# A Conformer trunk on one core: norms in one piece, a sixth plain chunk, pooling tiles as slices, ScalarE's tables asked for early

## The chip, the cores and the metric

The kernel runs on one core of one Trainium2 chip. The metric is the device time of an execution in microseconds; the median of three runs before the change is 1699.82 us (1695.87 to 1700.03). The core has TensorE (PE, with its weight loads shown as PEld), VectorE (DVE), ScalarE (ACT), GpSimd (POOL) and a DMA-issuing queue SP; each engine works off its own queue in order.

## The reference, cut to what matters

528 tokens (16 meta tokens and 512 frames) of 1024 channels pass through two Conformer layers, all in float32. The first layer mixes tokens by pooling, the second by latent attention over a key/value computed between the layers. Every sub-layer begins with an RMS norm.

```python
def rmsnorm(x, g):  x * rsqrt(mean(x*x, -1) + 1e-6) * g
def swiglu(h, w_gate, w_up, w_down):  (silu(h @ w_gate) * (h @ w_up)) @ w_down    # 1024 -> 2816 -> 1024
# layer l
h = h + 0.5 * swiglu(rmsnorm(h, ffn1_norm[l]), ...)
u = rmsnorm(h, mix_norm[l])
h = h + pool_mixer(u, pool_w, pool_scale)       # l == 0: trailing means over 2, 4, 8, 16 tokens
                                                # minus the token, a 256x256 map per channel group
h = h + mla_attention(u, ...)                   # l == 1: 8 heads, chunk-causal softmax(q k^T) v
h = h + 0.5 * swiglu(rmsnorm(h, ffn2_norm[l]), ...)
# after layer 0: shared k, v from rmsnorm(h, kv_in_norm); at the end rmsnorm(h, final_norm), meta dropped
```

## The kernel before, in words

Activations lie with channels on the 128 partitions and tokens along the free dimension: `h` is eight tiles of 128 x 528. Each float32 operand of a matmul is split in two fp32r parts, a high one (a rounded copy, made by ScalarE) and a low one (the remainder, made by VectorE); a product takes three matmuls, high x high, high x low and low x high (`mm3`, L193; `plain`, L371; `product`, L383). A weight of 512 KB comes from DRAM to a `raw` tile (two buffers), ScalarE copies its high part (L169), VectorE subtracts the remainder (L170), and the pair goes to two of 14 `w` tiles. `tp` holds 48 tiles of 128 x 528 for everything else.

The four feed-forwards (`ffn`) go over 22 chunks of 128 hidden units. A chunk's gate and up are made in one of two ways. *Plain* (`gate_up_plain`): 96 matmuls, from weights brought whole and split. *In sums* (`gate_up`): a Strassen-like scheme with 84 matmuls; it needs sums of weight halves, which DMA engines add on the way in (`bring_sums`: two loads on SP and an accumulating one on POOL) and VectorE completes (`add_up`, L421 and L422), and sums of halves of the input (`sums_x`, L245 to L248 and two splits for each of four channel pairs). `prepare` splits the forms of a chunk one ahead. Blocks of four or three chunks are then multiplied by the down weights, eight steps to a block (`down_steps`), put between the three slots of the chunks in sums of the following block; the last block's steps come at the end, and each step adds to one `h` tile (L614, L617).

Three feed-forwards have a norm of their own (`first_chunks`): chunk 0 runs on the unnormalised input and is scaled afterwards, so that the mean squares can be computed beside it. `rms[0]` makes the mean squares (L275), their powers on POOL and diagonal tiles (L292, L294); `rms[1]` broadcasts them (L303, L307). Chunk 1 still runs on the unnormalised input; `normal_x` (L224, then L183/L184 for the split) makes the normalised input piece by piece, from which chunk 2 on is computed, and from which `sums_x` is made. Before, chunks 0 to 4 are plain (`begun = 5`). The third feed-forward gets its normalised input from outside (`first_chunk`): the norm's broadcast is shared with the key/value projection (L811 to L829), its chunks 0 and 1 are plain.

The pooling mixer first applies the 256x256 maps (`z_products`, L734: tokens of tile j as the stationary operand), scales by the norm (`z_parts`, L740 and L741; mean squares in `z_scale`, L715), then applies band matrices over tokens (L766 to L778), adding to `h` at L780. Tokens come in tiles of 128; a fifth tile of 80 rows (`x5`, filled by POOL casts at L695, and `s5`) held the last 16 tokens of each half, apart from each other, in two groups.

Attention is one list of steps (`ATTENTION`): keys and queries of a head, values of a token tile, the scale for the scores (`scales`, L897 to L907), scores with their exponential (L990), normalising, transposing (`turn`, L1047) and weighing (L1065).

The order in which an engine runs its instructions is set when the kernel is built: a planner walks the program with its own model of times and issues, on each engine, what it holds to be ready, earlier lines first. So lines written later can come ahead of earlier ones that it thinks are not ready. ScalarE loads a function table when an activation of another set of functions comes up (Copy and Square need none of their own).

Of the kernel before, what the change touches and what calls it, by code (L numbers as in the profile page):

```python
# [11 lines left out]
F32 = mybir.dt.float32  # L12
# [46 lines left out]
B_0, B_4, B_M, NB = 0, 256, 528, 928  # L59
# [5 lines left out]
keys 0, values 1, scales, queries 0, values 3, queries 1, scores3 0, scores2 0, values 2, scores10 0, values 0,  # L65
# [15 lines left out]


def tail(ap):

    return ap.rearrange("p (a b) -> p a b", b=NM)[:, 15::17, :]


def spread(ap):

    return ap.rearrange("p (a b) -> p a b", b=64)[:, :, :NM]  # L90
# [3 lines left out]
def trunk(ctx: ExitStack, tc, h0, wall, vecs, band, rope, out):  # L94
# [26 lines left out]

    def psum():
        return psp.tile([P, 512], F32, tag="ps", name=name("ps"))
# [11 lines left out]
    nc.scalar.activation(warm, warm, AF.Copy)  # L135
# [45 lines left out]
    def split_to(dst, src):  # L181

        nc.scalar.activation(dst[0], src, AF.Copy)  # L183
        nc.vector.tensor_tensor(dst[1], src, dst[0], op=ALU.subtract)  # L184
# [33 lines left out]
    def normal_x(xs, c, g, t0, r):  # L218
# [112 lines left out]
    def fetch_gate_up(u0, one=fetch):  # L331
        one(u0)
        one(u0 + 1)

    def ffn(u0, x, g, rms, t0, after, early=None, final=None, normed=None, hooks=()):
# [56 lines left out]

        def pair_of_sums():
            return sump.tile([P, 2, 512], F32, tag="sum", name=name("sum"))
# [136 lines left out]
        def first_chunks():  # L531

            nonlocal x
# [16 lines left out]
            plain(w_g, pg, halves)  # L550
            r = rms[1]()
            fetch_gate_up(u0 + 6)
# [6 lines left out]
            fetch_gate_up(u0 + 9)  # L559
            sums_x(x, 0)  # L560
            gate_up_plain(2, True)
            fetch_gate_up(u0 + 12)
            sums_x(x, 1)
            sums_x(x, 2)
            gate_up_plain(3)
            bring_sums(5)
            bring(5)
            evacuate(0, *held, r)
            sums_x(x, 3)
            bring_sums(6)  # L570
            gate_up_plain(4, pair=True)
            prepare(5)
            bring(6)

        def first_chunk():
# [6 lines left out]
            for k in range(2):  # L582
                sums_x(x, k)
            gate_up_plain(1)
            for k in range(2, 4):
                sums_x(x, k)
            prepare(2)
# [38 lines left out]
        begun = 5 if normed is None else 2  # L626
# [42 lines left out]
    rows = [P, P, P, P, 80]  # L669
    x5, bands = [], []  # L670

    def early():
# [11 lines left out]
        for i in range(2):  # L684
            x5.append((slot(F32R)[:, :512], slot(F32R)[:, :512]))
            for t in x5[i]:
                nc.gpsimd.memset(t.bitcast(F32), 0.0)

    done = prep([(xm, V_MIX, 0)], ssq_m, 0)

    def after(c):
        done(c)
        for e in range(2):
            t = x5[c // 4][e][:, (c % 4) * P : (c % 4) * P + P]
            nc.gpsimd.tensor_copy(spread(t), tail(xm[c][e]))  # L695
# [5 lines left out]
    s5 = slot()[:, :P]  # L701
    nc.gpsimd.memset(s5, 0.0)
    nc.vector.tensor_copy(spread(s5), tail(ssq_m))

    def tokens(j, c, e):
        if j == 4:
            return x5[c // 4][e][:, (c % 4) * P : (c % 4) * P + 80]
        return xm[c][e][:, j * P : (j + 1) * P]

    def z_scale():  # L710

        ps = psum()
        for j in range(5):
            sj = s5[:, :80] if j == 4 else ssq_m[:, j * P : (j + 1) * P]
            nc.tensor.matmul(ps[: rows[j], 2 * j : 2 * j + 2], sj, ones_d, start=True, stop=True)  # L715
        v, rc = small(5), small(5)
        nc.vector.memset(v, 1.0)
        nc.vector.tensor_scalar(v[:, :4], ps[:, 0:8:2], EPS, None, op0=ALU.add)
        nc.vector.tensor_scalar(v[:80, 4:5], ps[:80, 8:9], EPS, None, op0=ALU.add)
# [563 lines left out]
```

## Time and profile before

| | before |
|---|---|
| median of three runs | 1699.82 us |
| the profiled execution's own time / its span | 1702.0 / 1700.2 us |
| mean granted TensorE clock | 0.981 |
| PE busy | 1637.3 us (96%), 11976 matmuls |
| DVE busy | 1142.5 us (67%) |
| ACT busy | 809.5 us (48%) |
| POOL busy | 221.9 us (13%) |
| read from HBM | 208 MB, 124 GB/s |

The span runs from the first to the last instruction of the profiled execution; its own time is 1.8 us longer. Busy times are sums over the span. Matmuls overlap their weight loads, and their ends are modelled. A granted clock of 1.00 is TensorE at 2.4 GHz; 0.5 would be 1.2 GHz throughout.

### The profile page before, as it was taken

To read this page: it belongs to the slowest core of one execution; us is meant where nothing else is said; L and a number is where in the kernel's file an instruction comes from. 1 tells how busy PE (TensorE), PEld (TensorE's weight loads), DVE (VectorE), ACT (ScalarE), POOL (GpSimd) and SP (SyncE) were. 2 spreads that over 40 slices of the span, in tenths; PEclk is the share of its full clock that TensorE was granted. 3 is DMA by queue.
4 is the path that set the end of the run, shared out by engine and by line. 5 is a ranking of instruction groups with operands and counts; after the bars stand their busy time and mean duration, and the time that the engine had idled before them with its cause. 6 is when DMAs were issued, how large, how long until landed. Compare 5 with 4: busy or idle time off the path is not lost.

```text
span 1700.2 us, 30059 instructions
## 1 busy us (share of the span) xinstructions
PE 1637.3 (96%) x11976; PEld 1555.5 (91%) x11976; DVE 1142.5 (67%) x1851; ACT 809.5 (48%) x1489; POOL 221.9 (13%) x257
## 2 busy tenths in 40 slices
PE   7999999998999999999899999999899899999997
PEld 7899999997999999999899999898787798999897
DVE  6865666657776566657767667566787766666655
ACT  6543444446454444445454444445576453444443
POOL 2000000005200000002000000001454100000002
PEclk9999999997999999999999999999899899999998
DMA  7455465533244555534355565643102434565411
GB/s 250 112 137 149 139 160 139 141 111 109 75 113 137 148 146 136 138 101 149 88 135 150 153 145 152 152 126 111 50 14 75 124 96 132 142 160 148 134 56 61
DMA packets 166206, 212.20 MB, mean 125 GB/s; under 512 B 10288, under 2 KB 102576, under 8 KB 166064
## 3 DMA queue, kind: packets, MB, share of 16 engines
q1 hardware_dynamic: 146176, 172.60, 32.2%
q0 software_dynamic: 19312, 37.23, 13.3%
q8 instruction: 94, 1.54, 0.4%
q10 hardware_dynamic: 576, 0.43, 0.1%
q14 instruction: 48, 0.39, 0.1%
HBM read 208.12 MB, written 2.10 MB: 124 GB/s over the span
## 4 chain that ended last, share of the span: by engine, by line
PE 84%; DVE 8%; DMA 3%; ACT 3%; issue 1%; POOL 0%; SPq 0%; DVEq 0%; ACTq 0%; POOLq 0%
PE ps L383 41%; PE ps L193 32%; PE ps L371 7%; DMA raw<-wall 2%; DVE t L184 2%; DVE t L224 1%; DVE w L170 1%; PE ps L1065 1%; DMA half<-wall 1%; ACT w L183 1%; DVE w L184 1%; PE ps L978 1%; PE ps L734 0%; PE ps L933 0%; ACT t L990 0%
## 5 line engine op out<-in xcount | busy, mean ns | idle before, releaser
L383 PE MATMUL ps<-t,w 128*128 128x256 f32 (+1 forms) x5964 | 757.1, 283 | 7.9 <-ACT t L525 6.7
L383 PEld LDWEIGHTS ps<-t,w 128*128 128x128 f32 x5964 | 740.1, 188 | 21.0 <-ACT t L525 8.1
L193 PE MATMUL ps<-t,w 128*128 128x264 f32 (+2 forms) x3672 | 628.4, 322 | 6.6 <-ACT t L183 2.0
L193 PEld LDWEIGHTS ps<-t,w 128*128 128x128 f32 x3672 | 527.9, 188 | 54.3 <-ACT t L183 5.0
L183 ACT ACTIVATE w<-half 128x512 fp32r<-128x512 f32 (+1 forms) x263 | 154.6, 603 | 230.8 <-PE ps L383 122.4
L371 PE MATMUL ps<-t,w 128*128 128x264 f32 (+1 forms) x1632 | 222.0, 297 | 21.5 <-DVE t L184 10.1
L371 PEld LDWEIGHTS ps<-t,w 128*128 128x128 f32 x1632 | 211.7, 199 | 30.1 <-DVE t L184 15.0
L403 POOL DMA_DIRECT2D sum<-wall x71 | 86.2, 1215 | 1077.9 <-DMA sum<-wall 400.6
L183 ACT ACTIVATE w<-sum 128x1024 fp32r<-128x1024 f32 x142 | 149.9, 1057 | 161.1 <-PE ps L383 108.2
L184 DVE TENSOR_TENSOR w<-half,w 128x512 fp32r<-128x512 f32 (+1 forms) x263 | 168.4, 655 | 70.6 <-ACT w L183 69.0
L184 DVE TENSOR_TENSOR w<-sum,w 128x1024 fp32r<-128x1024 f32 x142 | 173.1, 1220 | 54.3 <-PE ps L383 36.8
L614 DVE SCALAR_TENSOR_TENSOR h<-ps,h 128x528 f32<-128x528 f32 (+1 forms) x160 | 111.6, 697 | 140.1 <-PE ps L193 139.8
L183 ACT ACTIVATE t<-t 128x528 fp32r<-128x528 f32 (+4 forms) x174 | 99.0, 593 | 115.8 <-DVE t L526 62.9
L521 DVE TENSOR_TENSOR t<-ps,t 128x256 f32<-128x256 f32 (+1 forms) x71 | 30.3, 427 | 139.4 <-PE ps L383 138.5
L184 DVE TENSOR_TENSOR t<-t,t 128x528 fp32r<-128x528 f32 (+4 forms) x174 | 109.3, 643 | 11.2 <-ACT t L183 9.9
L184 DVE TENSOR_TENSOR w<-raw,w 128x1024 fp32r<-128x1024 f32 x71 | 86.7, 1221 | 28.1 <-PE ps L383 20.5
L183 ACT ACTIVATE w<-raw 128x1024 fp32r<-128x1024 f32 x71 | 74.9, 1055 | 55.5 <-PE ps L383 26.0
L170 DVE TENSOR_TENSOR w<-raw,w 128x1024 fp32r<-128x1024 f32 (+1 forms) x52 | 67.3, 1297 | 22.7 <-ACT w L169 21.1
L169 ACT ACTIVATE w<-raw 128x1024 fp32r<-128x1024 f32 (+1 forms) x55 | 54.5, 994 | 54.3 <-DMA raw<-wall 23.1
L263 POOL TENSOR_TENSOR t<-t,t 128x528 f32<-128x528 f32 (+1 forms) x33 | 52.9, 1603 | 156.4 <-ACT t L262 99.1
L513 ACT ACTIVATE t<-ps 128x256 f32<-128x256 f32 (+1 forms) x71 | 27.3, 385 | 81.8 <-PE ps L383 81.2
L211 DVE SCALAR_TENSOR_TENSOR t<-h,vt,t 128x528 fp32r<-128x528 f32 (+1 forms) x48 | 52.2, 1107 | 6.3 <-ACT t L210 6.1
(167 smaller groups left out, 1080.5 us busy)
## 6 DMA issues: line engine op xcount, KB each, us to landing
raw<-wall SPq DMA_DIRECT2D x118, 512.0 KB, 3.4
half<-wall SPq DMA_DIRECT2D x199, 256.0 KB, 3.8
sum<-wall SPq DMA_DIRECT2D x142, 256.0 KB, 3.2
sum<-wall POOLq DMA_DIRECT2D x71, 512.0 KB, 7.0
half<-wall SPq DMA_DIRECT2D x64, 192.0 KB, 2.8
h<-h SPq DMA_DIRECT2D x8, 264.0 KB, 5.6
raw<-wall SPq DMA_DIRECT2D x8, 256.0 KB, 4.0
raw<-band SPq DMA_DIRECT2D x4, 464.0 KB, 4.1
```

The source lines that it names most:

```text
L169: nc.scalar.activation(wh[:, a:b], raw[:, a:b], AF.Copy)
L170: low.tensor_tensor(wl[:, a:b], raw[:, a:b], wh[:, a:b], op=ALU.subtract)
L183: nc.scalar.activation(dst[0], src, AF.Copy)
L184: nc.vector.tensor_tensor(dst[1], src, dst[0], op=ALU.subtract)
L193: nc.tensor.matmul(ps, w[a], x[b][:, c0:c1], start=first and n == 0, stop=last and n == 2)
L211: nc.vector.scalar_tensor_tensor(xl, src, gain(g + c), xh, op0=ALU.mult, op1=ALU.subtract)
L263: (nc.vector if last else nc.gpsimd).tensor_tensor(ssq, ssq, sq, op=ALU.add)
L371: nc.tensor.matmul(ps, w[a][:, k * P : k * P + P], xs[k][i][b], start=k == 0 and n == 0, stop=k == KC - 1 and n == 2,)
L383: nc.tensor.matmul(ps, w[a][:, k * P : k * P + P], xs[k][b], start=first and k == 0 and n == 0, stop=last and k == 3 and n == 2, skip_grou ...
L403: nc.gpsimd.dma_start(t, up[:, :512].unsqueeze(1).to_broadcast([P, 2, 512]), accum_op=ALU.add)
L521: add(u[:, first], pd, u[:, first], op=ALU.add)
L614: nc.vector.scalar_tensor_tensor(hv, at, 0.5, hv, op0=ALU.mult, op1=ALU.add)
```

## The change

- ScalarE: the first instruction asks for Silu instead of Copy; a one-column Exp is added after the last square ahead of attention and a one-column Silu after the last residual of attention. They write a scratch tile.
- Pooling: the token tiles are the slices 0-128, 128-256, 240-368, 368-496 and 496-528 of the activations themselves; the casts, zeroed tiles and the copy of squares go; the band matrices have matching rows and columns.
- Feed-forwards with a norm: six plain chunks (`begun = 6`); the broadcast of the norm stands six eighths into chunk 1's gate. Everything traced after chunk 1's evacuation goes into a `tc.issue_after` block.
- Third feed-forward, pooling, attention: `tc.issue_after` blocks too. `with tc.issue_after(ins)` puts each instruction of the block that runs on the engine of `ins` behind `ins` in that engine's queue; it binds the order of issue on this one engine and nothing else. `xs["low"]`, `low` are VectorE instructions (the last remainder of the normalised input, of the pooled parts), `last` is a TensorE one (the last matmul of the score scale).
- Attention's list: `scales` moves from the third place to behind `values 3`, ahead of `queries 1`.

```diff
-keys 0, values 1, scales, queries 0, values 3, queries 1, scores3 0, scores2 0, values 2, scores10 0, values 0,
+keys 0, values 1, queries 0, values 3, scales, queries 1, scores3 0, scores2 0, values 2, scores10 0, values 0,
-    nc.scalar.activation(warm, warm, AF.Copy)
+    nc.scalar.activation(warm, warm, AF.Silu)
@@ normal_x
-            split_to(p, xn)
+            _, xs["low"] = split_to(p, xn)
@@ first_chunks
-            plain(w_g, pg, halves)
+            plain(w_g, pg, halves, range(6))
             r = rms[1]()
+            plain(w_g, pg, halves, range(6, KC))
             fetch_gate_up(u0 + 6)
             xs = new_x()
             for c in range(KC):
                 normal_x(xs, c, g, t0, r)
             plain(w_u, pu, halves)
             evacuate(1, by_halves(pg), by_halves(pu), r)
             x = xs
-            fetch_gate_up(u0 + 9)
...
-            gate_up_plain(3)
-            bring_sums(5)
-            bring(5)
-            evacuate(0, *held, r)
-            sums_x(x, 3)
-            bring_sums(6)
-            gate_up_plain(4, pair=True)
-            prepare(5)
-            bring(6)
+            with tc.issue_after(xs["low"].ins):
+                fetch_gate_up(u0 + 9)
+                sums_x(x, 0)
+                gate_up_plain(2, True)
+                fetch_gate_up(u0 + 12)
+                sums_x(x, 1)
+                sums_x(x, 2)
+                gate_up_plain(3)
+                fetch_gate_up(u0 + 15)
+                sums_x(x, 3)
+                gate_up_plain(4)
+                evacuate(0, *held, r)
+                bring_sums(6)
+                bring(6)
+                bring_sums(7)
+                gate_up_plain(5, pair=True)
+                prepare(6)
+                bring(7)
@@ first_chunk
+            with tc.issue_after(x["low"].ins):
+                for k in range(2):
+                    sums_x(x, k)
+                gate_up_plain(1)
+                for k in range(2, 4):
+                    sums_x(x, k)
+                prepare(2)
-        begun = 5 if normed is None else 2
+        begun = 6 if normed is None else 2
@@ pooling
-    rows = [P, P, P, P, 80]
+    spans = [(0, P), (P, 2 * P), (240, 368), (368, 496), (496, L)]
+    rows = [b - a for a, b in spans]
-            nc.gpsimd.tensor_copy(spread(t), tail(xm[c][e]))
     def tokens(j, c, e):
-        if j == 4:
-            return x5[c // 4][e][:, (c % 4) * P : (c % 4) * P + 80]
-        return xm[c][e][:, j * P : (j + 1) * P]
+        return xm[c][e][:, slice(*spans[j])]
-    fetch(U_FFN2_0, 2)
-    fetch(U_FFN2_0 + 1, 2)
+    with tc.issue_after(low.ins):
+        fetch(U_FFN2_0, 2)
+        fetch(U_FFN2_0 + 1, 2)
-        b_2, b_3 = bm[:, P : P + 272], bm[:, :272]
-        b_4 = b04[:80, B_4 : B_4 + 272]
+        b_2, b_3 = bm[:, P + 16 : P + 288], bm[:, 16:288]
+        b_4 = b04[: rows[4], B_4 : B_4 + 272]
@@ ahead of attention, in query_scales, behind attention
+    nc.scalar.activation(warm, ssq_c[:, :1], AF.Exp, scale=0.0)
-            nc.tensor.matmul(ps[:, 8 + 2 * j : 10 + 2 * j], ssq_c[:, ts], ones_q, start=True, stop=True)
+            last = nc.tensor.matmul(ps[:, 8 + 2 * j : 10 + 2 * j], ssq_c[:, ts], ones_q, start=True, stop=True)
+        order.enter_context(tc.issue_after(last.ins))
+    nc.scalar.activation(warm, h[KC - 1][:, NM : NM + 1], AF.Silu, scale=0.0)
```

## Rows read from the trace of the kernel before

**Rows 1.** The page's first part: busy us (share of the span) and instructions.

```profile
PE 1637.3 (96%) x11976; PEld 1555.5 (91%) x11976; DVE 1142.5 (67%) x1851; ACT 809.5 (48%) x1489; POOL 221.9 (13%) x257
```

**Rows 2.** Busy by stretch: us; PE, PEld, DVE, ACT, POOL; clock; DMA share; GB/s.

```profile
31.20:60.10 28.90, 23.77 (x152) 21.72 (x152) 25.06 (x47) 13.59 (x22) 1.24 (x1) 0.88 0.51 146
...
382.60:418.10 35.50, 27.45 (x167) 25.61 (x167) 27.53 (x36) 20.48 (x32) 20.43 (x25) 0.76 0.36 115
418.10:441.70 23.60, 23.60 (x197) 23.56 (x195) 17.56 (x28) 13.51 (x23) 9.52 (x6) 1.00 0.07 24
441.70:466.90 25.20, 24.70 (x196) 23.86 (x194) 21.57 (x47) 10.07 (x21) 2.42 (x2) 1.00 0.45 125
...
817.50:840.50 23.00, 17.81 (x110) 15.97 (x110) 22.32 (x50) 7.92 (x19) 1.74 (x2) 0.85 0.28 70
...
1336.50:1366.70 30.20, 25.73 (x147) 22.55 (x146) 25.75 (x51) 12.20 (x23) 1.28 (x1) 0.77 0.32 86
```

**Rows 3.** Chain of waits, first feed-forward: start us, us, what.

```profile
82.95 11.68 PE ps L383 x96
```

**Rows 4.** Timeline of PE, third feed-forward: start, us, engine, line, operation, count.

```profile
839.57 12.56 PE L371 MATMUL ps<-t,w 128*128 128x256 f32 x104
```

**Rows 5.** Timeline of the first feed-forward's norm.

```profile
31.16 6.60 PE L371 MATMUL ps<-t,w 128*128 128x264 f32 x52
...
33.95 0.76 DVE L224 SCALAR_TENSOR_TENSOR t<-h,vt,t 128x528 f32<-128x528 f32 x1
```

**Rows 6.** VectorE by line and shape, 31.2 to 60.1: count | busy, mean ns | idle.

```profile
L170 DVE TENSOR_TENSOR w<-raw,w 128x1024 fp32r<-128x1024 f32 x5 | 6.1, 1222 | 4.5 <-ACT w L169 4.5
L224 DVE SCALAR_TENSOR_TENSOR t<-h,vt,t 128x528 f32<-128x528 f32 x8 | 6.1, 760 | 0.0
L184 DVE TENSOR_TENSOR t<-t,t 128x264 fp32r<-128x264 f32 x8 | 3.2, 426 | 0.0
L184 DVE TENSOR_TENSOR t<-t,t 128x528 fp32r<-128x528 f32 x4 | 2.8, 698 | 0.0
...
L245 DVE TENSOR_TENSOR t<-t 128x264 f32<-128x264 f32 x4 | 1.7, 425 | 0.0
```

**Rows 7.** Chain of waits, fourth feed-forward.

```profile
1357.98 31.66 PE ps L371 x244
```

**Rows 8.** Timelines of PE and of VectorE there; in brackets idle time before, releaser.

```profile
1336.54 5.90 PE L371 MATMUL ps<-t,w 128*128 128x256 f32 x48
...
1339.15 0.69 DVE L421 TENSOR_TENSOR sum<-sum,raw 128x512 f32<-128x512 f32 x1 [3.45 <-DMA raw<-wall]
```

**Rows 9.** Timeline of PE, pooling.

```profile
389.11 2.34 PE L193 MATMUL ps<-t,w 128*128 128x264 f32 x18
...
403.47 1.87 PE L715 MATMUL ps<-ones_d,t 128*128 128x2 f32 x8 [2.54 <-DVE t L263]
...
418.20 0.28 PE L766 MATMUL ps<-t,t 128*128 128x256 f32 x1
```

**Rows 10.** POOL and VectorE by line, 382.6 to 418.1 (pooling).

```profile
L695 POOL CAST t<-t 128x32 fp32r<-128x32 f32 x16 | 10.3, 658 | 21.9 <-ACT t L210 19.7 <-DVE t L211 2.1
...
L170 DVE TENSOR_TENSOR w<-raw,w 128x1024 fp32r<-128x1024 f32 x4 | 6.7, 1678 | 0.3 <-ACT w L169 0.3
...
L170 DVE TENSOR_TENSOR w<-raw,w 128x512 fp32r<-128x512 f32 x4 | 3.6, 929 | 0.3 <-ACT w L169 0.3
```

**Rows 11.** Timeline of the start of attention.

```profile
1210.01 2.94 PE L193 MATMUL ps<-t,w 128*128 128x512 f32 x12
...
1212.80 0.28 PE L898 MATMUL ps<-ones_q,t 128*128 128x2 f32 x2
...
1219.75 1.28 ACT L990 ACT_TABLE_LOAD   x1
...
1221.05 0.79 ACT L990 ACTIVATE t<-ps,s,q 128x528 f32<-128x528 f32 x1
...
1224.67 2.33 PE L978 MATMUL ps<-t,t 128*128 128x256 f32 x9 [3.26 <-ACT t L990]
```

More of the change, by code (lines that the diff above doesn't have):

```diff
@@ L120, in unsplit, with pair_of_sums @@
         return rawp.tile([P, 1024], F32, tag="raw", name=name("raw"))
+    def pair_of_sums():
+        return sump.tile([P, 2, 512], F32, tag="sum", name=name("sum"))
     def psum():
@@ L181, in split_to @@
     def split_to(dst, src):
[L183 to L184 removed]
+        return (
+            nc.scalar.activation(dst[0], src, AF.Copy),
+            nc.vector.tensor_tensor(dst[1], src, dst[0], op=ALU.subtract),
+        )
     def parts(T):
@@ L328, in prep, with fetch_gate_up @@
         return after
-    def fetch_gate_up(u0, one=fetch):
-        one(u0)
-        one(u0 + 1)
+    def fetch_gate_up(u0):
+        fetch(u0)
+        fetch(u0 + 1)
     def ffn(u0, x, g, rms, t0, after, early=None, final=None, normed=None, hooks=()):
@@ L683, in early @@
             bands.append((b04, bm, bl))
[L684 to L694, printed above, removed]
-            nc.gpsimd.tensor_copy(spread(t), tail(xm[c][e]))
+    after = prep([(xm, V_MIX, 0)], ssq_m, 0)
     r0 = ssq
     ffn(U_FFN1_0, x, V_F1, rms_steps([r0], ones_d, L), 0, after, early)
-    s5 = slot()[:, :P]
-    nc.gpsimd.memset(s5, 0.0)
-    nc.vector.tensor_copy(spread(s5), tail(ssq_m))
     def tokens(j, c, e):
-        if j == 4:
-            return x5[c // 4][e][:, (c % 4) * P : (c % 4) * P + 80]
-        return xm[c][e][:, j * P : (j + 1) * P]
+        return xm[c][e][:, slice(*spans[j])]
     def z_scale():
@@ L713, in z_scale @@
         for j in range(5):
-            sj = s5[:, :80] if j == 4 else ssq_m[:, j * P : (j + 1) * P]
-            nc.tensor.matmul(ps[: rows[j], 2 * j : 2 * j + 2], sj, ones_d, start=True, stop=True)
-        v, rc = small(5), small(5)
+            nc.tensor.matmul(ps[: rows[j], 2 * j : 2 * j + 2], ssq_m[:, slice(*spans[j])], ones_d, start=True, stop=True)
+        v, rc, n = small(5), small(5), rows[4]
         nc.vector.memset(v, 1.0)
         nc.vector.tensor_scalar(v[:, :4], ps[:, 0:8:2], EPS, None, op0=ALU.add)
-        nc.vector.tensor_scalar(v[:80, 4:5], ps[:80, 8:9], EPS, None, op0=ALU.add)
+        nc.vector.tensor_scalar(v[:n, 4:5], ps[:n, 8:9], EPS, None, op0=ALU.add)
         for a, b in ((0, 2), (2, 5)):
@@ L1107, in trunk @@
     }
-    for step in ATTENTION.replace("\n", " ").split(","):
-        f, *args = step.split()
-        steps[f](*map(int, args))
+    with ExitStack() as order:
+        for step in ATTENTION.replace("\n", " ").split(","):
+            f, *args = step.split()
+            steps[f](*map(int, args))
     for d in range(KC):
```

33 lines of the change are left out of this document (7 added, 26 removed).

## The prediction

> **What bounds the kernel now.** First the page's busy times: TensorE is busy 1637.3 of 1700.2 us, VectorE 67%, ScalarE 48% [rows 1]. Inside the feed-forwards TensorE runs without gaps; what can be had is the 63 us in which it is idle, and the stretches in which its granted clock is low. Busy time by stretch finds them [rows 2]: the norm of the first feed-forward (TensorE 23.77 of 28.90 us, clock 0.88), the pooling mixer (27.45 of 35.50, clock 0.76), the norm of the third (17.81 of 23.00, 0.85) and of the fourth (25.73 of 30.20, 0.77). In these norms VectorE is the engine that is nearly full (25.06, 22.32, 25.75 us). In the second feed-forward, the same code, TensorE loses only 0.5 us (24.70 of 25.20). The timeline adds the start of attention, where TensorE waits 3.26 us for an exponential [rows 11].
>
> I price a stage by when its successor starts, which counts idle time and slow clock together. The chain of waits gives a matmul's price at full clock: 11.68/96 = 0.122 us with 528 tokens [rows 3], 12.56/104 = 0.120 with 512 [rows 4]. A plain chunk (96) is 11.7 or 11.5 us, a chunk in sums (84) 10.2 or 10.1.
>
> **First feed-forward: norms in one piece, six plain chunks, table.** Before: the plain matmuls end at 82.95; less chunks 3 and 4 (192 x 0.122 = 23.4), chunk 2 ended at 59.5. The chunk in sums behind it puts the start of chunk 6 at 82.95 + 84 x 0.122 = 93.2 [rows 3]. Chunk 1 had its matmuls done at 31.16 + 48 x 0.122 = 37.0 [rows 5], so chunk 2 took 22.5 us for 11.7 of work: it waited for normalised pieces. There VectorE did 6.1 + 3.2 + 2.8 us of norm, and between these the sums (four lines of 1.7), five weight remainders and add-ups [rows 6]. With the block queued behind the last norm remainder, VectorE does from 33.95 [rows 5] 12.1 of norm and the 2 remainders of chunk 2 (2.4), to 48.4; TensorE reaches the last of the eight pieces at 37.0 + 7 x 1.46 = 47.2. The broadcast, emitted 12 matmuls earlier, can bring this up to 1.5 us forward, so the lateness is between 0 and 1.2; I take 0.5. Four plain chunks are 46.8: 84.3. Chunk 3 needs PSUM banks that chunk 1 holds until VectorE evacuates it, now after the norms: 0 to 2 us, I take 1. Chunk 6 starts at 85.3: **-8**. Ends: -10 (no lateness) and -3 (next paragraph).
>
> What is late next is the work put off. From the norms to chunk 6 VectorE has, by the same lines: evacuations of chunks 1 and 0 (2.9 + 2.8), of 2 to 5 (4 x 1.5), six remainders (7.3), sums (10.6), forms of chunk 6 (5.4): 35 us, against 288 x 0.122 = 35.1 of TensorE. It is level. In the second feed-forward's norm VectorE managed 21.57 of 25.20, 86% [rows 2], which would make it 41; but some 6 us of the list (evacuations of 5 and 0, the last forms) isn't wanted when chunk 6 starts. The cover is just there; without it 5 us are lost, which is the -3. Down steps of the first block fall on six slots instead of nine, two to a slot: nothing, TensorE having other products to put between; at worst 2 us a feed-forward for the one pair of banks. SP: the sum loads are for chunks 6 and 7 instead of 5 and 6; chunk 5 brings 1 MB instead of 1.5, POOL issues one summing transfer less.
>
> **Fourth feed-forward, the same edit.** 31.66 us of plain matmuls ran without a gap from 1357.98, to 1389.6 [rows 7]; chunk 2 ended at 1389.6 - 192 x 0.119 = 1366.8. Chunk 1 was done at 1336.54 + 48 x 0.12 = 1342.3. VectorE came late to the norms because an add-up of chunk 5 sat in its queue, waiting 3.45 us for a transfer [rows 8]; that add-up now lies in the block. Wait and add-ups gone, the norms start near 1338, 11.7 us of pieces, to 1349.7, and TensorE wants the last at 1352.4: no lateness. Chunk 6: before 1389.6 + 10.1 = 1399.7, after 1342.3 + 4 x 11.4 = 1387.9, with 2 us for banks and debt 1390: **-9.5** (ends -11.5, -4).
>
> **Second feed-forward.** Half a microsecond to win, and 12 matmuls more: **+1** (0 to +3).
>
> **Third feed-forward.** The first chunk ended 104 - 96 = 8 matmuls after 839.57, at 840.5 [rows 4]. VectorE was full for 22.32 of 23.00 us [rows 2], and sums (6.8), two forms (2.4) and add-ups (1.4) lay between its norms. Without them the chunk ends at 834 to 835. But these 10.6 us are due before the next chunk's 11.5 us are over, and VectorE has other evacuations there, so some 2.5 comes back: **-3.5** (0 to -6).
>
> **Pooling.** 167 matmuls at 0.122 are 20.4 us of the 35.5 [rows 2]: 15 us are lost. The last down step ends at 391.4, the mean squares begin at 403.47 after a wait for the last square, the band matmuls at 418.20 [rows 9]. In between POOL has 16 casts of tails, 10.3 us, in one queue with the six square additions, and VectorE 6.7 + 3.6 us of weight remainders of the next feed-forward [rows 10]. Slices take the casts away; the issue order puts the remainders behind the last pooled part. Then the last residual comes at about 392.4, its split and its square's addition by 396, mean squares and powers 3 to 4 us, the ten parts at 0.65 from 399.9, the last four products between them: band matmuls at about 406, -12. Against this stands the debt: in the stretch that follows VectorE is busy 17.56 of 23.60 [rows 2], 6 us free for 10.3 of remainders. I give back 4: **-8**. Ends: -14 (no debt, no idle time), -2 (the products wait for part after part and the clock stays low). ScalarE's halves of these weights are not held, only VectorE's. Slices of 32 instead of 80 rows leave the moving columns as they are: nothing.
>
> The Trainium skill (SBUF — State Buffer, "SBUF: two separate sides") says that a VectorE operation with two SBUF inputs and a POOL operation that reads SBUF lock each other out for a whole instruction. The remainder takes 1.68 us here and 1.22 in the first norm [rows 6, 10], which agrees. By that rule the casts' going shortens VectorE's pieces too, which lies within the -14.
>
> **Attention.** The score scale's matmuls stand behind 12 query matmuls of 0.23 us [rows 11]; with *scales* ahead of *queries 1* nine of these follow them: 2.1 us. The table load, 1.28 us, stands right ahead of the first exponential [rows 11]; asked for at the last square, it falls into idle time of ScalarE, 1.3 if not. TensorE's wait of 3.26 us goes with these 3.4, and the nine matmuls moved behind fill part of it either way: **-2.5** (0 to -3.4). Everything on TensorE later in the list is now queued behind the scale; if the last square is late, TensorE waits, and up to the 2.1 won is lost. The two silu loads lie in evacuations counted above; the new request after attention stands behind the last split on ScalarE, at nothing (1.3 if ahead of it).
>
> The Trainium skill (ScalarE: Activation LUTs, "What ACT_TABLE_LOAD costs") adds a drain of 1.38 us to the load's 1.28. The exponential starts 1.30 us after the load began [rows 11], so no drain shows here. By the page, as an estimate, attention would give 1.4 us more.
>
> **Sum.** -8 + 1 - 3.5 - 8 - 2.5 - 9.5 = -30.5 on the profiled execution's 1702.0: 1671.5. The median of the runs is 2.2 us below that execution: 1669.
>
> **Rivals.** (1) *Half of it*: weights come late. For: a raw buffer is freed by its remainder, and remainders now wait for the norms or the pooled parts, so the next transfer does too. Against: a plain chunk leaves 11.5 us for two weights. If it decides in both norms and in pooling, half of these goes: 4 + 4.7 + 4 given back, 1682.
> (2) *VectorE's debt decides* (slower): the 35 us put off ahead of chunk 6 run below 86%, because VectorE waits in order for ScalarE's halves. Three feed-forwards then lose 3 x (35/rate - 35.1), which at a rate of 0.78 takes all of the 30.5; at 0.73 it is 38.5, 8 more than the gains: 1708. Against: 86% was reached.
> (3) *It doesn't do what it says*: the edges bind one engine's queue each, VectorE's in the norms; the planner may still set work traced earlier between the norms (remainders of chunk 2, the evacuation of 1) and order the other engines worse. Then casts, table and scale alone count, -7, against 4.4 for 36 matmuls: 1697.
> (4) *All of it*: the far ends, -10 + 0 - 6 - 14 - 3.4 - 11.5 = -45: 1655.
>
> **Numbers.** Forecast 0.56, (1) 0.21, (2) 0.07, (3) 0.08, (4) 0.08. The forecast's own range is 1660 to 1680. The whole range leaves out (2), (3) and half of (4): 1654 to 1692. A measurement here can tell 0.3%, 5 us. Faster: the forecast, (1), (4) = 0.85. Same: most of (3) = 0.07. Slower: (2) and the rest of (3) = 0.08.
>
> **What would show it.** Norm pieces back to back on VectorE; chunk 2 of the first feed-forward over by 51, with TensorE at full clock; no casts, and band matmuls 15 to 19 us behind the last down step instead of 27; three table loads, none ahead of an activation that is waited for; TensorE idle some 40 us instead of 63. Wrong would be: TensorE waiting for VectorE's forms ahead of chunk 6, or for banks ahead of chunk 3; a gap in the plain matmuls behind pooling.

## The result, and the profile after

After: 1671.43 us median of 4 runs (1669.28 to 1672.74); before, beside it on the same chip: 1698.65 (1695.87 to 1700.03). The ratio is 0.9841, 95% interval 0.9823 to 0.9858: 27 us less, where 1669 was forecast. The profiled execution took 1671.36 us (span 1669.2), 30.6 us less than the one of before. The difference between 27 and 30.6 is the execution profiled before: at 1702.0 us and a granted clock of 0.981 it lay 3.4 us above its kernel's median here, while the one after lies at its median. So the stages below add up to some 3 us more than the kernel gained.

The page's first part, after [rows 1]:

```profile
PE 1623.6 (97%) x12012; PEld 1544.8 (93%) x12012; DVE 1129.2 (68%) x1832; ACT 801.1 (48%) x1472; POOL 210.6 (13%) x233
```

TensorE is idle for 1669.2 - 1623.6 = 45.6 us instead of 62.9. The 36 matmuls more are the sixth plain chunks of three feed-forwards. The helper lines have moved: a plain chunk's matmuls are L366, those in sums L378, the splits L177 (ScalarE) and L178 (VectorE), weight remainders L163, norm pieces L219.

Busy by stretch, after [rows 2]; the columns are the stretch, its us, then PE, PEld, DVE, ACT, POOL, the granted clock, DMA share and GB/s:

```profile
31.20:60.10 28.90, 28.90 (x238) 28.87 (x238) 26.45 (x52) 14.56 (x26) 0.00 (x0) 1.00 0.26 93
384.60:399.00 14.40, 12.45 (x102) 11.71 (x100) 10.85 (x17) 6.63 (x11) 5.72 (x5) 1.00 0.00 1
...
802.40:820.70 18.30, 16.02 (x110) 15.07 (x111) 16.06 (x34) 7.28 (x16) 0.00 (x0) 0.91 0.19 33
1315.50:1336.10 20.60, 19.54 (x160) 18.71 (x158) 17.47 (x35) 8.61 (x16) 0.00 (x0) 1.00 0.13 47
```

In the first norm TensorE issues 238 matmuls where it issued 152, and its clock is full (0.88 before). Pooling, from the last down step to the band matmuls, lasts 14.5 us (384.5 to 399.00) instead of 26.8 (391.4 to 418.20), at full clock.

The timeline of PE ahead of the first feed-forward's plain run, its chain of waits, and the timeline of PE in the fourth [rows 3, 7]:

```profile
23.96 6.17 PE L366 MATMUL ps<-t,w 128*128 128x264 f32 x36
```

```profile
31.34 54.30 PE ps L366 x444
85.64 5.59 PE ps L378 x46
```

```profile
1315.54 12.69 PE L366 MATMUL ps<-t,w 128*128 128x256 f32 x102
1328.81 0.50 PE L366 MATMUL ps<-t,w 128*128 128x256 f32 x2 [0.58 <-ACT t L177]
1329.54 40.91 PE L366 MATMUL ps<-t,w 128*128 128x256 f32 x340 [0.22 <-DVE t L178]
```

In the first feed-forward the rest of chunk 1 and four whole plain chunks are one unbroken run, and chunk 6 starts at 85.64 instead of 93.2. In the fourth two short waits are left, and the plain run ends at 1370.45.

A stage is priced by the start of what follows it, before against after, so that idle time and clock count together. The starts of chunk 6 before (93.2, 501.6, 1399.5) are worked out: the end of the plain run and 84 matmuls; the others are rows, to about 0.2 us:

| stretch | foreseen | measured | from |
|---|---|---|---|
| first feed-forward to chunk 6 | -8 | -7.6 | 93.2 to 85.64 |
| its rest, to the last down step | 0 | +0.7 | 391.4 to 384.5 |
| pooling, to the first band matmul | -12 | -12.3 | 418.20 to 399.00, less 6.9 |
| band matmuls and second feed-forward to chunk 6 | +4 and +1 | +3.2 | 501.6 to 485.56, less 19.2 |
| the second's rest, to the key and value mean squares | 0 | +0.5 | 810.78 to 795.27, less 16.0 |
| third feed-forward | -3.5 | -0.5 | 1172.80 - 810.78 to 1156.78 - 795.27 |
| attention | -2.5 | -2.4 | 1316.65 - 1172.80 to 1298.23 - 1156.78 |
| fourth feed-forward to chunk 6 | -9.5 | -10.6 | its start 18.4 sooner, chunk 6 (1399.5 to 1370.45) 29.05 |
| its rest | 0 | -2.3 | 1659.85 to 1628.53 at the last stage |

Together that is -31.3; behind the last of these marks 0.7 us are lost, which makes the 30.6.

### The profile page after: what moved, and what is told of

Same layout as the page of the kernel before. It is cut to its first block, busy times and chain, and to the rows that moved or that the text cites. A ratio compares the mean times of both kernels' runs of the same rounds, so it can differ in the third digit from the quotient of the medians.

```text
span 1669.2 us, 30003 instructions
## 1 busy us (share of the span) xinstructions
PE 1623.6 (97%) x12012; PEld 1544.8 (93%) x12012; DVE 1129.2 (68%) x1832; ACT 801.1 (48%) x1472; POOL 210.6 (13%) x233
## 4 chain that ended last, share of the span: by engine, by line
PE 87%; DVE 6%; ACT 3%; DMA 2%; issue 1%; POOL 1%; SPq 0%; DVEq 0%; ACTq 0%; POOLq 0%
PE ps L378 39%; PE ps L188 32%; PE ps L366 12%; DMA half<-wall 1%; DVE t L178 1%; PE ps L1052 1%; ACT w L177 1%; DVE w L178 1%; DVE t L219 1%; DVE t L206 1%; PE ps L965 1%; DVE w L163 1%; ACT t L177 1%; PE ps L716 0%; PE ps L270 0%
## 5 line engine op out<-in xcount | busy, mean ns | idle before, releaser
L378 PE MATMUL ps<-t,w 128*128 128x256 f32 (+1 forms) x5712 | 726.3, 283 | 9.1 <-ACT t L517 5.7
L378 PEld LDWEIGHTS ps<-t,w 128*128 128x128 f32 x5712 | 709.0, 188 | 22.9 <-ACT t L517 7.2
L177 ACT ACTIVATE w<-half 128x512 fp32r<-128x512 f32 (+1 forms) x260 | 153.1, 603 | 228.6 <-PE ps L378 104.0
L366 PE MATMUL ps<-t,w 128*128 128x264 f32 (+1 forms) x1920 | 241.9, 288 | 9.9 <-ACT w L162 5.2
L366 PEld LDWEIGHTS ps<-t,w 128*128 128x128 f32 x1920 | 237.6, 192 | 12.4 <-ACT w L162 5.2
L177 ACT ACTIVATE w<-sum 128x1024 fp32r<-128x1024 f32 x136 | 143.5, 1058 | 159.5 <-PE ps L378 116.7
L178 DVE TENSOR_TENSOR w<-half,w 128x512 fp32r<-128x512 f32 (+1 forms) x260 | 166.8, 655 | 71.8 <-ACT w L177 70.4
L395 POOL DMA_DIRECT2D sum<-wall x68 | 82.2, 1215 | 1052.1 <-DMA sum<-wall 424.6
L178 DVE TENSOR_TENSOR w<-sum,w 128x1024 fp32r<-128x1024 f32 x136 | 165.7, 1220 | 29.4 <-PE ps L378 16.8
L177 ACT ACTIVATE t<-t 128x528 fp32r<-128x528 f32 (+4 forms) x174 | 99.0, 594 | 104.1 <-DVE t L518 66.1
L178 DVE TENSOR_TENSOR t<-t,t 128x528 fp32r<-128x528 f32 (+4 forms) x174 | 109.1, 646 | 20.6 <-ACT t L177 19.0
L178 DVE TENSOR_TENSOR w<-raw,w 128x1024 fp32r<-128x1024 f32 x68 | 83.1, 1222 | 27.0 <-PE ps L378 21.1
L177 ACT ACTIVATE w<-raw 128x1024 fp32r<-128x1024 f32 x68 | 71.8, 1056 | 54.3 <-PE ps L188 25.6
L162 ACT ACTIVATE w<-raw 128x1024 fp32r<-128x1024 f32 (+1 forms) x61 | 60.7, 1000 | 59.2 <-DMA raw<-wall 40.5
L258 POOL TENSOR_TENSOR t<-t,t 128x528 f32<-128x528 f32 (+1 forms) x33 | 55.2, 1673 | 216.7 <-ACT t L257 159.1
L163 DVE TENSOR_TENSOR w<-raw,w 128x1024 fp32r<-128x1024 f32 (+1 forms) x58 | 71.5, 1239 | 9.1 <-ACT w L162 8.4
L206 DVE SCALAR_TENSOR_TENSOR t<-h,vt,t 128x528 fp32r<-128x528 f32 (+1 forms) x48 | 54.4, 1154 | 8.7 <-ACT t L205 8.6
```

Source lines behind the costliest of these rows:

```text
L162: nc.scalar.activation(wh[:, a:b], raw[:, a:b], AF.Copy)
L163: low.tensor_tensor(wl[:, a:b], raw[:, a:b], wh[:, a:b], op=ALU.subtract)
L177: nc.scalar.activation(dst[0], src, AF.Copy),
L206: nc.vector.scalar_tensor_tensor(xl, src, gain(g + c), xh, op0=ALU.mult, op1=ALU.subtract)
L258: (nc.vector if last else nc.gpsimd).tensor_tensor(ssq, ssq, sq, op=ALU.add)
L366: nc.tensor.matmul(ps, w[a][:, k * P : k * P + P], xs[k][i][b], start=k == 0 and n == 0, stop=k == KC - 1 and n == 2,)
```

## The experiments

Each ratio below is to runs of the kernel before that were made beside the kernel in question. The medians of these runs were 1698.54, 1698.26 and 1697.61 us in three groups, so that times of different groups compare to about 1 us.

### The issue order in the first chunks

```diff
-            with tc.issue_after(xs["low"].ins):
-                fetch_gate_up(u0 + 9)
-                ...
+            fetch_gate_up(u0 + 9)
+            ...
```

> The changed kernel without the issue order in the first chunks of the feed-forwards one, two and four; six plain chunks and everything else stay. Theory: the order is what makes the norm pieces run back to back. Without it sums and remainders come between them again, chunk 6 of the first feed-forward starts 7 to 10 us later (93 to 96 instead of 85.6), that of the fourth 8 to 12 later behind the start of its plain chunks, time 1686 to 1693. Rival: the sixth plain chunk is what pays, by giving VectorE time for sums and forms; then most of the gain stays and the time is 1671 to 1677.

1691.3 us (ratio to before 0.9951, 0.9934 to 0.9967): 20 of the 27 us are gone. The timeline of PE in its first feed-forward shows the old gaps:

```profile
31.65 16.11 PE L366 MATMUL ps<-t,w 128*128 128x264 f32 x124
48.77 2.10 PE L366 MATMUL ps<-t,w 128*128 128x264 f32 x12 [1.01 <-DVE t L178]
52.96 2.11 PE L366 MATMUL ps<-t,w 128*128 128x264 f32 x12 [2.08 <-DVE t L178]
55.55 36.26 PE L366 MATMUL ps<-t,w 128*128 128x264 f32 x296 [0.48 <-DVE t L178]
91.64 4.54 PE L378 MATMUL ps<-t,w 128*128 128x264 f32 x36
```

TensorE waits for the remainders of norm pieces, and behind each wait 12 matmuls take 2.10 us instead of 1.46. Chunk 6 starts 6.2 us later, a little less than the 7 to 10 expected. From the start of the fourth feed-forward to its chunk 6 it is 82.1 us (1308.55 to 1390.66) instead of 72.06, and in the second it is 63.3 instead of 59.95 from the end of the mean squares' matmuls to chunk 6. These are 6 + 3 + 10 of the 20. The theory holds: without the order the pieces no longer run back to back. The rival (the sixth chunk pays by itself) falls.

### Five plain chunks instead of six

```diff
-        begun = 6 if normed is None else 2
+        begun = 5 if normed is None else 2
-                fetch_gate_up(u0 + 15)
-                sums_x(x, 3)
-                gate_up_plain(4)
+                bring_sums(5)
+                bring(5)
                 evacuate(0, *held, r)
+                sums_x(x, 3)
                 bring_sums(6)
-                bring(6)
-                bring_sums(7)
-                gate_up_plain(5, pair=True)
-                prepare(6)
-                bring(7)
+                gate_up_plain(4, pair=True)
+                prepare(5)
+                bring(6)
```

> The changed kernel with five plain chunks instead of six in the feed-forwards one, two and four (the issue order stays): 12 matmuls fewer in each, 4.4 us in all, and one plain chunk less to hide the 35 us of VectorE work put off behind the norms. Theory of the prediction (the cover is just there with six, and about 5 us each would be lost without it in the first and fourth): in both TensorE waits for VectorE's forms ahead of and behind the first chunk in sums, 3 to 6 us each, in the second 0 to 3; time 1673 to 1680. Rival (VectorE has room, the sixth chunk only costs its 12 matmuls): 1667.

1686.28 us (0.9926, 0.9909 to 0.9943), worse than the 1673 to 1680 expected. PE's timeline from the plain run of the first feed-forward on, and ScalarE's and VectorE's ahead of the first wait:

```profile
31.45 42.69 PE L366 MATMUL ps<-t,w 128*128 128x264 f32 x348
73.98 5.64 PE L378 MATMUL ps<-t,w 128*128 128x264 f32 x45
82.27 0.39 PE L378 MATMUL ps<-t,w 128*128 128x264 f32 x1 [2.66 <-ACT t L177]
83.10 4.71 PE L378 MATMUL ps<-t,w 128*128 128x264 f32 x24 [0.44 <-DVE t L178]
```

```profile
77.03 1.15 ACT L177 ACTIVATE w<-half 128x512 fp32r<-128x512 f32 x2 [2.03 <-PE ps L378]
...
80.24 0.71 DVE L455 TENSOR_TENSOR t<-t,t 128x528 f32<-128x528 f32 x1
...
81.05 1.71 ACT L177 ACTIVATE t<-t 128x528 fp32r<-128x528 f32 x3 [2.33 <-DVE t L455]
```

The plain run is as dense as in the changed kernel, and then TensorE waits for the sums of x, split too late. In the profiled executions the band matmuls begin 4.7 us later than in the changed kernel though 12 matmuls (1.5 us) are left out; from there to the mean squares of the key and value stage it is 2.3 us longer, from the start of the fourth feed-forward to the end 4.0. So the arrangement with the sixth chunk buys about 6, 4 and 5 us for 1.5 each. (This profiled execution was the fastest of its kernel, 1683.05 us; the other three, at a lower granted clock, took 2.4 to 4.2 us more, and no trace shows where.)

Whether it is the chunk's length that pays is not shown by this run alone, because the edit changes the order too: it puts `sums_x(x, 3)` behind the evacuation of chunk 0, where the changed kernel has it ahead. The wait falls just there. ScalarE first waits 2.03 us for TensorE ahead of writing a weight tile; then chunk 0 is evacuated (its last step is VectorE's L455), and only behind that come the three splits on which TensorE waits, by their order in the source that of chunk 0 and the two of the last sums of x. VectorE itself idled for 1.15 us of this time, waiting for ScalarE. In the changed kernel the last of these splits is done by 70, 15 us ahead of chunk 6. Five chunks with `sums_x(x, 3)` ahead of the evacuation would tell the length from the order; no run has that.

In the changed kernel, from VectorE's last norm remainder (45.1) to chunk 6 (85.5), VectorE was busy for 35.6 of 40.4 us, 88%. So the put-off work fits under six plain chunks with little to spare, near the prediction's 86%.

### Pooling: the hold on VectorE's remainders

```diff
-    with tc.issue_after(low.ins):
-        fetch(U_FFN2_0, 2)
-        fetch(U_FFN2_0 + 1, 2)
+    fetch(U_FFN2_0, 2)
+    fetch(U_FFN2_0 + 1, 2)
```

> The changed kernel without the issue order behind the pooled parts (VectorE may do the next feed-forward's two weight remainders, 10.3 us in the kernel before, ahead of them); slices instead of casts stay. Theory: of the 12.3 us by which the band matmuls come sooner, the larger part is the casts' going, 7 to 9, and the hold gives 3 to 5: band matmuls at 402 to 404 instead of 399.0, some of it returned behind them since VectorE then has less to do; time 1672 to 1675. Rival: the hold gives most of it, band matmuls at 407 or later, time 1677 to 1681. Second rival: the planner puts the remainders behind the pooled parts by itself, and nothing changes.

1678.59 us (0.9878, 0.9863 to 0.9892). Band matmuls start at 405.70, 6.7 us later; the chain of waits runs through the remainders again:

```profile
387.66 1.13 DVE w L163
388.80 0.68 DVE t L206
389.47 2.27 DVE w L163
...
394.07 1.12 DVE w L163
395.21 0.70 DVE t L258
395.96 2.08 PE ps L697 x10
```

They stand ahead of the splits (L206) and of the last square's addition (L258), on which the mean squares wait; then TensorE runs at 1.2 instead of 2.4 GHz (granted clock 0.50 from 394.5 to 399.0). Of the 12.3 us the hold gives 6.7; the other 5.6 are left, by difference, to the slices (the casts' going and what goes with them). The start of the band matmuls lies between theory and rival, the time is the rival's: the hold is worth more than the theory gave it. Nothing of the 6.7 comes back behind (plain run at 437.96 instead of 431.22), which the theory had wrong.

### Rows of the last pooling tile

```diff
-    spans = [..., (368, 496), (496, L)]
+    spans = [..., (368, 496), (400, L)]
-  ... = entries(s + 496, np.arange(256, 528)[None], w, True)
+  ... = entries(np.where(s < 96, -1000, s + 400), np.arange(256, 528)[None], w, True)
```

> The changed kernel with its last pooling tile widened from 32 to 128 rows (tokens 400 to 527, band rows of tokens below 496 zero); everything else is left, VectorE's and ScalarE's instructions too. Theory (short weight loads): the two band matmuls per channel whose stationary operand has 32 rows start 0.2 us and more behind their predecessor instead of 0.12; eight channels of 1.72 us return to 1.35, so chunk 6 of the second feed-forward starts 2.5 to 3 us sooner behind the first band matmul (83.9 instead of 86.56 us), and the time falls to about 1668.7. Rival (the prediction's own: VectorE's put-off remainders hold TensorE back behind pooling): 86.5 stays, time 1671.4. A third possibility, that 128 rows of zeros cost TensorE something of their own, would show as over 86.6.

> The last pooling tile with 64 rows (tokens 464 to 527, band rows below 496 zero). If any matmul of fewer rows than its neighbours starts late, the eight channels stay near 1.72 us each; but the 80 rows of the kernel before started 0.12 behind their predecessor, so if it is a matter of how short the load is, 64 rows lie on one side or the other: 1.35 us per channel if only the 32-row load is late, 1.7 if 64 rows are late too.

One channel's band matmuls in the changed kernel (32 rows in the last tile), from the last with 128 rows, then the same with 64 rows and with 128 (timelines of PE):

```profile
399.94 0.28 PE L760 MATMUL ps<-t,t 128*128 128x272 f32 x1
400.15 0.39 PE L761 MATMUL ps<-t,t 32*128 32x272 f32 x1
400.38 0.28 PE L762 MATMUL ps<-t,t 32*128 32x272 f32 x1
400.60 0.38 PE L750 MATMUL ps<-t,t 128*128 128x256 f32 x1
```

```profile
399.74 0.29 PE L760 MATMUL ps<-t,t 128*128 128x272 f32 x1
399.96 0.39 PE L761 MATMUL ps<-t,t 64*128 64x272 f32 x1
400.19 0.28 PE L762 MATMUL ps<-t,t 64*128 64x272 f32 x1
```

```profile
402.18 0.29 PE L760 MATMUL ps<-t,t 128*128 128x272 f32 x1
402.30 0.29 PE L761 MATMUL ps<-t,t 128*128 128x272 f32 x1
402.43 0.29 PE L762 MATMUL ps<-t,t 128*128 128x272 f32 x1
```

With 128 rows every start is 0.12 us behind the one before; with 32 and with 64 rows the short matmuls, and the two behind them, come 0.21 to 0.23 behind. The weight loads of these instructions in the changed kernel, then at the change to 80 rows in the kernel before (timelines of PEld), show where the time goes:

```profile
399.82 0.19 PEld L760 LDWEIGHTS ps<-t,t 128*128 128x128 f32 x1
400.15 0.18 PEld L761 LDWEIGHTS ps<-t,t 32*128 32x128 f32 x1
400.26 0.18 PEld L762 LDWEIGHTS ps<-t,t 32*128 32x128 f32 x1
400.59 0.19 PEld L750 LDWEIGHTS ps<-t,t 128*128 128x128 f32 x1
```

```profile
419.06 0.19 PEld L776 LDWEIGHTS ps<-t,t 128*128 128x128 f32 x1
419.18 0.19 PEld L777 LDWEIGHTS ps<-t,t 80*128 80x128 f32 x1
```

At each change between 128 and 32 rows the load starts 0.33 us behind the load ahead of it, elsewhere 0.11 to 0.13, the change to 80 rows included: two late loads in each of eight channels. With 128 rows throughout, the eight channels take 10.7 us (401.22 to 411.93) instead of 13.7. Yet the time is 1671.51 (0.9837, 0.9822 to 0.9851): nothing gained. So the theory holds for the band matmuls and the rival for the time. Two things took the 3 us. VectorE is now the later one: the next feed-forward's first plain matmuls wait for its splits and take 14.1 us instead of 11.8 up to the mean squares:

```profile
418.23 7.65 PE L366 MATMUL ps<-t,w 128*128 128x264 f32 x56 [1.11 <-DVE t L206]
```

And in this run the last 24 pooling products took 4.63 us instead of 3.06, the granted clock being 0.57 from 396.7 to 399.0. So chunk 6 of the second feed-forward starts 1.7 us later (487.10 to 485.39); attention, in which the clock fell less, gives 1.6 back. The single run with 64 rows took 1674.4 us, and its channels 1.73 us each, as with 32: 64 rows are late too.

### VectorE's next remainders put back as well

```diff
-            fetch_gate_up(u0 + 3)
+            with tc.issue_after(split_x.low.ins):
+                fetch_gate_up(u0 + 3)
```

on the kernel with 128 rows; `split_x.low` is the last remainder of the feed-forward's input.

> The kernel with 128 rows in the last pooling tile, and besides VectorE's two remainders for the weights of chunk 1 (3.5 us at 411 to 416, ahead of the last splits of the second feed-forward's input) put behind the last of these splits. With 128 rows the band matmuls took 10.7 us instead of 13.7, but TensorE then waited for a split and its first chunk took 2.4 us longer. Theory (two waits lie beside each other here, TensorE's short weight loads and VectorE's remainders; only taking both away pays): first band matmul to the norm's broadcast in the second feed-forward 28.4 to 29 us instead of 31.2 (128 rows alone: 30.7), time about 1668.5 to 1669.5. Rival (VectorE is simply full there, what is put off returns one step later): 30.5 and 1671.5. In the first and fourth feed-forwards the same order should do nothing, or bring the norm forward by less than 1 us.

1672.48 us (0.9844, 0.9829 to 0.9859): no gain. The first plain chunk has no wait any more (11.7 us to the mean squares), but what was put off returns one step on, as the rival said, though smaller:

```profile
424.59 1.36 PE L366 MATMUL ps<-t,w 128*128 128x264 f32 x9
426.75 4.03 PE L366 MATMUL ps<-t,w 128*128 128x264 f32 x31 [0.80 <-ACT t L537]
```

From the first band matmul (401.15) to the broadcast (430.69) it is 29.5 us, instead of 30.4 with 128 rows alone and 30.9 in the changed kernel: 1.4 gained on the latter, less than expected, and the last pooling products again took 4.63 us, at a granted clock of 0.64 from 396.7 to 399.0, which costs as much.

### The third feed-forward

```diff
-            with tc.issue_after(x["low"].ins):
-                for k in range(2):
-                ...
+            for k in range(2):
+            ...
```

> The changed kernel without the issue order in the third feed-forward alone. In the changed kernel the first chunk there ended 4.3 us sooner than before (as foreseen) but of the 3.5 us foreseen only 0.5 was left by the start of attention: TensorE waited for VectorE's put-off sums and forms at 840 to 870. Theory (the gain is handed back there, the work being due before it can be hidden): without the order the first chunk ends some 4 us later and attention begins 0 to 1 us later behind the key and value projection, 377.5 to 378.5 us instead of 377.46; time 1671.4 to 1672.5. Rival (the order saves the foreseen 3.5, and something else in this feed-forward got worse by 3): 381 us, time 1675.

1677.65 us (0.9879, 0.9856 to 0.9902; two runs). From the mean squares of the key and value stage to the query projections it is 364.0 us (796.40 to 1160.38) instead of 361.5 (795.27 to 1156.78). The order saves 2.5 us, so my theory that all of it is handed back is wrong. (The two runs lie 5 and 8 us above the changed kernel's median; the profiled one, the faster, starts this stage 1.1 us late as well, and its last 1.3 us stay open.) Of the 4.3 us that it saves up to the end of the first chunk (825.16 instead of 819.68, less the later start of 1.1), 2.8 are returned by 873. A further part of the missing term lies elsewhere: in the changed kernel, as in this one and in the one without the pooling hold, TensorE waits near 1117 for an evacuation behind a down weight that came late (chain of waits of the changed kernel):

```profile
1108.14 7.32 DMA half<-wall
...
1116.70 1.32 PE ps L378 x9
```

The kernel before has no such wait there; it costs 0.9 us in the changed kernel, 1.1 and 1.6 in the two others, and 0.2 in the next one. Why this transfer comes late was not settled.

```diff
-        begun = 6 if normed is None else 2
+        begun = 6 if normed is None else 3
...
+                fetch_gate_up(u0 + 6)
                 ...
                 gate_up_plain(1)
...
+                gate_up_plain(2)
-                prepare(2)
+                prepare(3)
```

> The changed kernel with three plain chunks instead of two in the third feed-forward (12 matmuls, 1.4 us more) and one plain chunk's 11.5 us in which VectorE can do the sums and forms that the issue order puts off. If the put-off work is what gives the gain back (2.7 us at 840 to 870), the waits go and attention begins 375.5 to 376.5 us behind the key and value projection instead of 377.46: time 1669.5 to 1670.5. If the waits there have another source (weights, banks), the 1.4 us come on top: 379, time 1673.

1669.76 us (0.9834, 0.9817 to 0.9852). The debt is gone: behind the third plain chunk the chunks in sums run through, where the changed kernel waited 1.26 us:

```profile
835.30 11.62 PE L366 MATMUL ps<-t,w 128*128 128x256 f32 x96 [0.35 <-ACT t L448]
846.76 17.20 PE L378 MATMUL ps<-t,w 128*128 128x256 f32 x144
```

```profile
841.30 0.76 PE L378 MATMUL ps<-t,w 128*128 128x256 f32 x5
843.32 0.98 PE L378 MATMUL ps<-t,w 128*128 128x256 f32 x6 [1.26 <-DVE t L178]
```

The third feed-forward takes 357.9 us (796.08 to 1153.95) instead of 361.5 in spite of 12 matmuls more: 3.6 us, more than the 1 to 2 expected; 0.7 of it is the shorter wait for the late transfer. In the profiled execution 2 of it are lost again in the fourth feed-forward, 1.1 of these at its first plain chunk, where TensorE waits 0.82 us for the last square's addition on VectorE; the rest stays open. The time, 1.7 us less by the medians, can't be told from the changed kernel's.

### Attention: table and scale

```diff
-    nc.scalar.activation(warm, warm, AF.Silu)
+    nc.scalar.activation(warm, warm, AF.Copy)
...
-    nc.scalar.activation(warm, ssq_c[:, :1], AF.Exp, scale=0.0)
...
-    nc.scalar.activation(warm, h[KC - 1][:, NM : NM + 1], AF.Silu, scale=0.0)
```

> The changed kernel without the early requests for ScalarE's tables (the first activation a copy again, no exponential asked for at the last square, no silu after attention); the score scale stays where it is. Theory (the load of 1.28 us stood on the path to the first exponential): attention, from the run of query projections to the first plain chunk of the fourth feed-forward, 142.5 to 142.8 us instead of 141.45, and up to 1.3 us more where the silu table is loaded in the fourth feed-forward's first evacuation; time 1672.5 to 1674. Rival (with the scale's matmuls moved forward TensorE has other work there, and the load costs nothing): 141.5, time 1671.4.

```diff
-keys 0, values 1, queries 0, values 3, scales, queries 1, ...
+keys 0, values 1, scales, queries 0, values 3, queries 1, ...
-        order.enter_context(tc.issue_after(last.ins))
```

> The changed kernel with the score scale back in its old place and without the issue order behind its last matmul; the early table requests stay. Theory (nine query matmuls of 0.23 us stood ahead of it): attention 143.4 to 143.7 us instead of 141.45, that is 2.1 longer; time 1673.5. Rival (the planner puts the matmuls ahead by itself, or the moved matmuls fill the wait either way): 141.5 to 142, time 1671.4 to 1672.

Without the requests: 1674.29 us (0.9863, 0.9846 to 0.9879), attention 142.9 us (1157.60 to 1300.46). With the scale in its old place: 1670.19 (0.9838, 0.9823 to 0.9852), attention 140.0 (1158.29 to 1298.30), not longer but shorter. The time with the old place is 1.2 us below the changed kernel's by the medians and 0.5 by the ratios, so not to be told from it; that without the requests is 2.9 above by the medians, 1.4 of which is attention. ScalarE ahead of the first exponential, without the requests and then with the scale put back:

```profile
1204.12 0.37 ACT L177 ACTIVATE t<-ps 16x256 fp32r<-16x256 f32 x1 [1.50 <-PE ps L919]
1204.51 1.28 ACT L976 ACT_TABLE_LOAD   x1
1205.81 0.79 ACT L976 ACTIVATE t<-ps,s,q 128x528 f32<-128x528 f32 x1
```

```profile
1204.79 0.37 ACT L177 ACTIVATE t<-ps 16x256 fp32r<-16x256 f32 x1 [1.50 <-PE ps L919]
1205.07 0.77 ACT L976 ACTIVATE t<-ps,s,q 128x528 f32<-128x528 f32 x1
```

Behind the start of the query projections the exponential begins at 48.25 before [rows 11], at 48.21 without the requests, at 46.78 with the old scale and at 46.66 in the changed kernel. The table makes the difference, and the scale's place next to none. The exponential stands in ScalarE's queue behind an evacuation of values that waits 1.50 us for TensorE, which has run 205 matmuls by then wherever the scale's small ones stand among them. What else differs is the clock. With the old scale it falls once ahead of the exponential (0.70 and 0.73 from 1190.2 to 1196.2). In the changed kernel it falls there too (0.62 and 0.82 from 1194.7 to 1200.7) and once more further on (0.78 and 0.65 from 1262 to 1268, where with the old scale it is 1.00): that second fall is the 1.4 us between 140.0 and 141.45. In the kernel with 128 rows, with the same instructions, the first fall is missing; the exponential begins at 45.06, and attention takes 139.8.

### Both improvements

> The changed kernel with 128 rows in the last pooling tile and three plain chunks in the third feed-forward. By the runs of each alone, the second brings 1.6 us (3.6 in the third feed-forward itself) and the first 0 (its shorter band stage is given back); time 1669 to 1670, not to be told from the changed kernel. If the clock does not fall in the last pooling products here (1.5 us in the run with 128 rows alone), 1668.

1669.40 us (0.9833, 0.9818 to 0.9848). By the medians it is the fastest, 2 us below the changed kernel, as expected and under what can be told here. In its profiled execution the clock did not fall in the last pooling products, for which 1668 had been expected.

## Why the prediction was right, and where not

**First and fourth feed-forward, right.** -7.6 for -8 and -10.6 for -9.5. The norm pieces need no wait of TensorE in the first, and chunk 3 waits for no bank, so the 1.5 us set aside for these were not spent. That the number came out even so is luck: the broadcast, emitted 12 matmuls earlier, did not come earlier (31.2 before and after), because ahead of it 36 matmuls took 6.0 us (23.96 to 29.96), at a granted clock of 0.84 from 20 to 31 instead of 1.00. The level sum of 35 us against 35.1 is borne out as far as that VectorE was busy for 35.6 of 40.4 us and TensorE waited for none of it. That without the sixth chunk 5 us are lost came out in size (6, 4 and 5), but that run changed the order too, so that its cause is argued and not shown. The 2.3 us in the rest of the fourth were not foreseen; 1.2 of them are less idle time of TensorE (2.0 instead of 3.1 us), the others stay open.

**Second feed-forward.** That there was only half a microsecond to win held for the kernel as it was. With six plain chunks the order is needed there too: without it 3.3 us are lost.

**Pooling, right in size, in part for the wrong reason.** -12.3 came where -12 stood, and the run without the hold splits it. Two terms failed, and hid each other. "Slices of 32 instead of 80 rows ... nothing" counted moving columns only, and the short stationary tiles cost 3 us in the band matmuls. The debt of 4 given back did not show: it lay beside the slow matmuls, and 2.3 us of it came out as soon as these were quicker. That the sum of both, 3.2, fell close to the 4 and 1 foreseen is luck.

**Third feed-forward, mis-sized.** -0.5 for -3.5. "Some 2.5 comes back" was right (2.7 to 2.8 by 870). The term that was too large is the gain ahead of it: 4.3 us at the chunk's end, where 5.5 to 6.5 were foreseen. With the sums gone from between the norms TensorE still waits 2.7 us for pieces there, and its clock is 0.91. A further 0.9 is the late transfer, for which no term stood.

**Attention, right in sum, wrong in its parts.** The 2.1 us for the score scale were worth nothing that shows, since it didn't set the exponential's start. The table gave 1.4 to 1.5 where 1.3 was set, and behind the shorter wait (1.76 instead of 3.26 before) TensorE's clock stays at 1.00 in the changed kernel, where without the requests (a wait of 3.27) it is 0.54 from 1210.5 to 1213.5. In the run without the requests the exponential again begins 1.30 us after the load does (1204.51, 1205.81). The Trainium skill (ScalarE: Activation LUTs, "What ACT_TABLE_LOAD costs") states a drain on top of the load; none shows in any run here.

**The sum.** Its terms miss by more than the total does: the third feed-forward gave 3.0 less than foreseen, the fourth with its rest 3.4 more. And the median was to lie 2.2 us below the profiled execution, as before; after the change it lies at it, which is most of what parts 1671.4 from 1669.

**Rivals.** (1) and (3) did not happen: the remainders' buffers delayed nothing in the norms, and the order kept the norms clear. Of (2) something shows in the third feed-forward (2.8 us) and, with 128 rows, behind pooling (2.3 us). Its own sum at a rate of 0.78 comes to 29.3 us, not to all of the 30.5, which changes nothing in the argument.

## What to carry to other kernels

When an order puts work off, add up that work on the engine which does it and compare it with the time until it is due: the gain lasts only where cover stands ahead, and cover (here a chunk in a longer but simpler form) can be bought: in the third feed-forward a third plain chunk of 12 matmuls more brought 3.6 us there. A wait that TensorE no longer has is worth more than its length where the clock falls behind it, and a step that merely moves ahead in one queue is worth nothing if the waiter stands in another queue behind something else. After taking away one of two waits that lie beside each other, look for the second before calling the first harmless.

## What the runs showed of the hardware

Among stationary tiles of 128 rows, those of 32 and of 64 rows were loaded late, and so was the first of 128 behind them: 0.33 us behind the load ahead instead of 0.12. Tiles of 80 rows in the kernel before were not (0.12). With 16 short matmuls in eight groups that cost 3 us.

Equal instructions with equal waits met different clocks. Two kernels waited 1.79 and 1.78 us for the same pooled part: the one with 128 rows went on at 0.57 for 2.3 us and took 4.63 us for the next 24 products, the one with both improvements took 3.12 us for them. After the scale's small matmuls the clock fell in the changed kernel and not in the one with 128 rows. Such a fall costs about 1.5 us each time, so that a stage's difference of that size in one execution says little by itself.
